# A decoder layer's start: the first adaLN columns move from VectorE to TensorE, and the small vectors ride with x

## The chip, the cores and the metric

The kernel runs on one core of a Trainium2 chip. A core has five engines with a queue each: TensorE (PE in the profile; PEld is its loading of the stationary operand), VectorE (DVE), ScalarE (ACT), GpSimd (POOL) and SyncE (SP, which here only issues transfers), and 16 DMA engines that move data between the chip's memory and the on-chip buffers. Times are device microseconds of the program, the median of several runs.

## The reference

The layer works on 256 rows of 1,024 numbers. A conditioning vector c gives, through one big matrix, nine groups of 1,024 numbers (shift, scale and gate of three sub-layers); each sub-layer normalises, scales and shifts its input, and its output is gated and added back.

```
mod = (silu(c) @ w_ada + b_ada)                      # 9 x 1024 numbers: sh1 sc1 gt1 sh2 ...
sh1, sc1, gt1, sh2, sc2, gt2, sh3, sc3, gt3 = split(mod, 9)
n = rmsnorm(h, g_ffn1) * (1 + sc1) + sh1
h = h + 0.5 * gt1 * ((silu(n @ w1_gate) * (n @ w1_up)) @ w1_down)
n = rmsnorm(h, g_mix) * (1 + sc2) + sh2
h = h + gt2 * hybrid_mixer(n)                        # pooling + dilated attention
n = rmsnorm(h, g_ffn2) * (1 + sc3) + sh3
h = h + 0.5 * gt3 * swiglu(n, w2_gate, w2_up, w2_down)
return rmsnorm(h, g_final)
```

All inputs are float32. Each large product is made of three TensorE products of rounded parts, so every weight tile is first split into `hi` (rounded, a cast) and `lo` (what the rounding lost, a subtraction), and so is every activation tile (`nh`, `nl`).

## The kernel before

**One stream of weights.** All weights lie in memory as 114 units of 128 x 2,048 numbers (1 MB each), in the order in which they are used (`plan`). `fetch` issues the transfer of one unit from SP into one of four buffers `raw` (L274). A unit of kind `ada` holds two blocks of 128 columns of `w_ada`, turned so that a column of the result lies on a partition: VectorE multiplies each block (128 x 1,024) with `cb`, the vector silu(c) repeated on all partitions, and sums along the row (L279), which gives two columns of `mod`. Any other unit is cast to `hi` by ScalarE (L290) and subtracted to `lo` by VectorE (L291), and its buffer is then free for the next transfer.

**The first feed-forward, one k-tile at a time.** The first products cannot wait for all of `mod`. So the first eight k-tiles (j = 0 to 7, 128 of the 1,024 inputs each) are done one after the other: an `ada` unit gives the shift and scale columns of tile j, `scale_cols` makes the factor `acol` (L377), `lead_mod` applies both to the transposed normalised rows and gives `nha` and `nla` (L463 to L466), and `lead_step` makes 24 products of 512 columns (L485) with the `lead` unit of the same j. Units 0 and 1 (tile 0) and 2 and 3 (tile 1) are the first four of the stream.

**The start, in a written order.** Tile 0 is written out by hand inside `in_order()` (L550 to L591), which makes each engine keep the order of the text. TensorE runs short products without use (`spin`), spreads c over the partitions (`pc`, L554), and turns the first halves of the normalised rows of both row tiles (`xt`, L318). VectorE squares and sums the rows (L561), makes `gains` (L567), the two columns of `mod` from unit 0 (L570), `acol` (L377), the first cast of unit 1 (L579), `n32` and `nla` (L582, L584), and the four `lo` pieces of unit 1 (L590). ScalarE scales the rows (L534), makes `nha` (L581), and casts the rest of unit 1 (L587) with two copies of turned rows between (L537). Behind it `casts_after` holds the casts of later units back.

**The small vectors.** The biases of `w_ada`, the three gains and `pool_scale`, 100 numbers on each partition, come as a tile of their own, `vecs`, by a transfer that ScalarE issues at the start (L204). The rows x come in two transfers from SP (L201, L203).

**Elsewhere.** The order of the rest comes from a scheduler that places instructions by priority; GpSimd issues the transfers of the mixer's tables (L775 to L777) and makes the inverse roots of the norms.

Of the kernel before, what the change touches and what calls it, by code (L numbers as in the profile page):

```python
# [15 lines left out]
P = 128  # L16
S = 256
NT = S // P
D = 1024
# [23 lines left out]
WMIX = (4, 12)  # L43
WLEAD = (0, 4)
RAW = 4
SPIN = (4, 8, 8, 5)
SPLIT = (9, 10)
GATE = 25
PARTS = 11
PAD = 336  # L50


def lead_set(f, j):
# [48 lines left out]
def pack(inp):  # L102
    def f(name):
        return np.asarray(inp[name])

    adaT = f("w_ada")[0].T.reshape(NMOD * KD, P, D)
    gu, down = [], []
    for i in (1, 2):
        g = f(f"w{i}_gate")[0].reshape(KD, P, NCH, 256)
        u = f(f"w{i}_up")[0].reshape(KD, P, NCH, 256)  # L110
        gu.append(np.stack([g, u], axis=3))
        down.append(f(f"w{i}_down")[0].reshape(NCH, 2, P, D))
    win = f("w_in")[0].reshape(2, 4, P, 4, 512)
    wout = f("w_out")[0].reshape(4, 2, P, D)
    order = plan()
    w = np.empty((len(order), P, 2048), np.float32)
    for i, (kind, a) in enumerate(order):
        if kind == "ada":
            w[i].reshape(P, 2, D)[:] = adaT[list(a)].transpose(1, 0, 2)
        elif kind == "lead":  # L120
            w[i].reshape(P, LEAD, 2, 256)[:] = gu[a[0]][a[1], :, list(lead_set(*a))].transpose(1, 0, 2, 3)
        elif kind == "gu":
            w[i].reshape(P, 4, 2, 256)[:] = gu[a[0]][4 * a[2]:4 * a[2] + 4, :, a[1]].transpose(1, 0, 2, 3)
        elif kind == "down":
            w[i].reshape(P, 2, D)[:] = down[a[0]][a[1]].transpose(1, 0, 2)
        elif kind == "win":
            w[i].reshape(P, 4, 512)[:] = win[a[1], :, :, a[0]].transpose(1, 0, 2)
        else:
            w[i].reshape(P, 2, D)[:] = wout[a].transpose(1, 0, 2)

    vec = np.concatenate([
        f("b_ada")[0].reshape(NMOD * KD, P).T,
        f("g_ffn1")[0].reshape(KD, P).T,
        f("g_mix")[0].reshape(KD, P).T,
        f("g_ffn2")[0].reshape(KD, P).T,
        f("pool_scale")[0].reshape(4, P).T,
    ], axis=1)
    x = f("x")[0].reshape(NT, P, D).transpose(1, 0, 2).reshape(P, NT * D)
    wpool = f("w_pool")[0].transpose(1, 0, 2).reshape(P, 4 * P)
    return {  # L140
        "w": w, "vec": np.ascontiguousarray(vec), "x": np.ascontiguousarray(x),
        "c": np.ascontiguousarray(f("c")), "gf": np.ascontiguousarray(f("g_final")).reshape(1, D),
        "wpool": np.ascontiguousarray(wpool), "band": band(), "bias": bias_table(),
    }
# [28 lines left out]
def block_kernel(ctx, tc, w, vec, x, c, gf, wpool, bandd, biasd, out):  # L173
# [18 lines left out]

    ffn1_pool = tc.tile_pool(name="ffn1", bufs=1, reuse_waits="tile")
    fp = [ffn1_pool.__enter__()]
    h = const.tile([P, NT * D], F32, name="h")
    cb = const.tile([P, D], F32, name="cb")
    ident = const.tile([P, P], F32, name="ident")
    lay.tile([P, PAD // 4], F32, name="lay")
    crow = work.tile([P, D], F32, name="crow", tag="gt", bufs=1)[0:1, :]
    vecs = const.tile([P, vec.shape[1]], F32, name="vecs")  # L200
    nc.sync.dma_start(h[:, 0:D], x[:, 0:D])  # L201
    nc.scalar.dma_start(crow, c)
    nc.sync.dma_start(h[:, D:2 * D], x[:, D:2 * D])  # L203
    nc.scalar.dma_start(vecs, vec)  # L204

    G1, PS = NMOD * KD, NMOD * KD + 3 * KD
    mod = const.tile([P, NMOD * KD], F32, name="mod")
    acol = const.tile([P, 3 * KD], F32, name="acol")
    make_identity(nc, ident)
    gains = const.tile([P, 3 * KD], F32, name="gains")  # L210
    mhalf = const.tile([P, 1], F32, name="mhalf")
    nc.gpsimd.memset(mhalf, -0.5)
    deps = const.tile([P, 1], F32, name="deps")
    nc.gpsimd.memset(deps, D * EPS)
    ones = work.tile([KD, P], F32, name="ones", tag="gs", bufs=1)[0:1, :]
# [53 lines left out]
    def fetch():  # L269
        i = pos[0]  # L270
        pos[0] += 1
        kind, a = order[i]
        raw = rawp.tile([P, 2048], F32, name=f"raw{i}", tag="raw")
        nc.sync.dma_start(raw, w[i])  # L274
        if kind == "ada":
            with tc.high_priority(offset=ADA if i >= 2 * KD else 0):
                for s, m in enumerate(a):
                    r = raw[:, ts(s, D)]
                    note(nc.vector.tensor_tensor_reduce(  # L279
                        r, r, cb, 1.0, vecs[:, m:m + 1], ALU.mult, ALU.add, mod[:, m:m + 1]), i, 1)  # L280
                    done_mod.add(m)
            return
        his, los = [], []
        for s in range(2):
            hi = hip.tile([P, 1024], F32R, name=f"hi{i}_{s}", tag="hi")
            lo = lop.tile([P, 1024], F32R, name=f"lo{i}_{s}", tag="lo")
            n = 1024 // (2 if i in (1, 2 * KD - 1) else 1)
            for o in range(0, 1024, n):
                src = raw[:, s * 1024 + o:s * 1024 + o + n]
                note(nc.scalar.copy(hi[:, o:o + n], src), i + s / 2, 0)  # L290
                note(nc.vector.tensor_tensor(lo[:, o:o + n], src, hi[:, o:o + n].bitcast(F32), ALU.subtract), i + s / 2, 0)  # L291
                casts[order[i], s] = bulk[-2][0].ins, bulk[-1][0].ins
            his.append(hi)
            los.append(lo)
        ready[(kind, a)] = (his, los)
# [233 lines left out]
    def spin(n):  # L529
        for _ in range(n):  # L530
            mm(spin_ps, spin_in[:, 0:P], spin_in, start=True, stop=True)

    def x_rows(t, b):
        return nc.scalar.activation(xs[t][:, ts(b, 512)], h[:, t * D + b * 512:t * D + b * 512 + 512], AF.Copy, scale=rs[t])  # L534

    def x_keep(t, b, pt):
        nc.scalar.copy(xT[b][:, :, ts(t, P)], pt)  # L537

# [11 lines left out]
    with in_order() as last:  # L550
        spin(SPIN[0])
        for b in range(2):
            pc = psp.tile([P, 512], F32, name=f"pc{b}", tag="ps")
            mm(pc, ones, crow[:, ts(b, 512)], start=True, stop=True)  # L554
            nc.scalar.activation(cb[:, ts(b, 512)], pc, AF.Silu)
        for t in range(NT):
            spin(SPIN[1 + t])
            xs.append(hip.tile([P, D], F32, name=f"xs{t}", tag="hi"))
            v = tiny.tile([P, 1], F32, name=f"vx{t}", tag="v")
            ht = h[:, ts(t, D)]  # L560
            nc.vector.tensor_tensor_reduce(xs[t], ht, ht, 1.0, D * EPS, ALU.mult, ALU.add, v)  # L561
            rs.append(tiny.tile([P, 1], F32, name=f"rx{t}", tag="r"))
            nc.gpsimd.tensor_tensor(rs[t], v, mhalf, ALU.pow)
            x_rows(t, 0)
            turned.append(turn(xs[t][:, 0:512], f"xt{t}0"))
        spin(SPIN[3])
        nc.vector.tensor_scalar(gains, vecs[:, G1:PS], float(D) ** 0.5, None, ALU.mult)  # L567
        for s, m in enumerate(order[0][1]):
            r = raw[0][:, ts(s, D)]
            nc.vector.tensor_tensor_reduce(r, r, cb, 1.0, vecs[:, m:m + 1], ALU.mult, ALU.add, mod[:, m:m + 1])  # L570
            done_mod.add(m)
        scale_cols(0, SC1, 0, 1)
        a, sh = acol[:, 0:1], mod[:, SH1 * KD:SH1 * KD + 1]
        n32 = work.tile([P, S], F32, name="n32l00", tag="t2", bufs=T2)
        for q in range(4):
            src = raw[1][:, ts(q, 512)]
            hi, lo = his[q // 2][:, ts(q % 2, 512)], los[q // 2][:, ts(q % 2, 512)]
            if q == 0:
                nc.vector.tensor_copy(hi, src)  # L579
                for t in range(NT):  # L580
                    nc.scalar.activation(n1[t][0][:, 0, :], turned[t][:, 0, :], AF.Identity, bias=sh, scale=a)  # L581
                    nc.vector.tensor_scalar(n32[:, ts(t, P)], turned[t][:, 0, :], a, sh, ALU.mult, ALU.add)  # L582
                for t in range(NT):
                    nc.vector.tensor_tensor(n1[t][1][:, 0, :], n32[:, ts(t, P)], n1[t][0][:, 0, :].bitcast(F32),  # L584
                                            ALU.subtract)
            else:
                nc.scalar.copy(hi, src)  # L587
                if q < 3:
                    x_keep(q - 1, 0, turned[q - 1])
            nc.vector.tensor_tensor(lo, src, hi.bitcast(F32), ALU.subtract)  # L590
# [105 lines left out]
    bias = [xp.tile([P, 4 * S], F32, name="bias0")]  # L696
    band_all = xp.tile([P, 4, 2 * P + 16], F32, name="band_all")
    wp_all = xp.tile([P, 4 * P], F32, name="wp_all")
    nc.gpsimd.dma_start(bias[0], biasd[:, 0:4 * S])

    def scores(hp):
# [52 lines left out]
    def pool_group(g, u, y):  # L754
# [8 lines left out]
        p2 = psp.tile([P, S], F32, name=f"pw{g}", tag="ps")  # L763
        mm(p2, wp, pl, start=True, stop=True)
        with urgent():
            sc = vecs[:, PS + g:PS + g + 1]
            for t in range(NT):
                nc.scalar.activation(y[t][0][:, g, :], p2[:, ts(t, P)], AF.Copy, scale=sc)
            for t in range(NT):
# [3 lines left out]
    after = finish1(1)  # L773
    bias.append(work.tile([P, 4 * S], F32, name="bias1", tag="gt", bufs=1))
    nc.gpsimd.dma_start(bias[1], biasd[:, 4 * S:8 * S])  # L775
    nc.gpsimd.dma_start(band_all, bandd)
    nc.gpsimd.dma_start(wp_all, wpool)  # L777
    QS = -DH ** -0.5
    y = [new_n(f"y{t}") for t in range(NT)]
    z = {}  # L780
# [167 lines left out]
```

## Time and profile before

| | |
|---|---|
| time, median of 3 runs (range) | 481.24 us (480.64 to 481.9) |
| the profiled execution: time, span | 481.04 us, 479.2 us |
| TensorE busy, share of the span | 469.0 us, 98% |
| weight loads of TensorE | 381.2 us, 80% |
| VectorE busy | 355.8 us, 74% |
| ScalarE busy | 260.9 us, 54% |
| bytes moved, mean rate | 126.05 MB, 263 GB/s |

The span is what the trace covers; the program's time has 1.84 us around it. A chain of waits goes back from the last instruction to what released each step. In a timeline each row has the start, the length, the engine, the line, the operation with what it writes and reads, how many instructions are merged in the row, and in brackets how long the engine had idled and what ended that.

### The profile page before, as it was taken

The page shows a single profiled execution, that of the slowest core. Times are in us where ns is not written, and L with a number is a line of the kernel's source. Part 1 is how long each engine was busy: PE and PEld are TensorE (multiplying, and loading weights), DVE is VectorE, ACT ScalarE, POOL GpSimd, SP SyncE. Part 2 cuts the span into 40 slices and gives each one's busy share as a digit, 9 for nine tenths or more (in the row PEclk, how much of TensorE's full clock was granted, in tenths as well). Part 3 has the DMA queues.
Part 4 walks back from the last instruction along what each step waited for, and adds up shares of the span by engine and source line. Part 5 has one row for each costly group of instructions (what it writes and reads, how often), then busy time and mean ns, then how long its engine had stood idle before and what let it go on. Part 6 is the DMA issues. An engine that isn't in the chain of part 4 may idle for free.

```text
span 479.2 us, 6028 instructions
## 1 busy us (share of the span) xinstructions
PE 469.0 (98%) x2188; PEld 381.2 (80%) x2188; DVE 355.8 (74%) x577; ACT 260.9 (54%) x447; POOL 13.4 (3%) x35
## 2 busy tenths in 40 slices
PE   8999999999999999999999999999999999999994
PEld 4678888888888888888878888888878888888883
DVE  4988899996987893789999868946666855655244
ACT  3686585454454460896877288845643543444121
POOL 1000000000000000110001000000000000000010
PEclk9999999999999999999999999999999999999998
DMA  8999995998988892579878944985457648630102
GB/s 302 412 349 345 358 347 186 351 420 356 351 316 329 302 379 122 221 279 377 334 284 334 346 177 178 376 324 176 176 180 271 260 191 327 230 122 0 44 1 88
DMA packets 19215, 126.05 MB, mean 263 GB/s; under 512 B 2329, under 2 KB 2865, under 8 KB 4850
## 3 DMA queue, kind: packets, MB, share of 16 engines
q1 hardware_dynamic: 17568, 121.12, 66.5%
q0 software_dynamic: 1184, 3.98, 2.4%
q10 hardware_dynamic: 434, 0.58, 0.3%
q8 instruction: 17, 0.28, 0.2%
q14 instruction: 12, 0.10, 0.1%
HBM read 124.61 MB, written 1.06 MB: 262 GB/s over the span
## 4 chain that ended last, share of the span: by engine, by line
PE 88%; ACT 5%; DMA 3%; issue 1%; DVE 1%; POOL 0%; POOLq 0%; DVEq 0%
PE accf L437 22%; PE gu L396 18%; PE gu L397 9%; PE le L485 9%; PE ld L485 8%; PE accm L829 5%; PE zp L396 4%; DMA raw<-in_w_dram 3%; PE zp L397 2%; PE ht L422 2%; ACT hi L290 2%; PE ld L396 2%; PE sh L396 2%; ACT nhb L367 1%; ACT n32b L368 1%
## 5 line engine op out<-in xcount | busy, mean ns | idle before, releaser
L291 DVE TENSOR_TENSOR lo<-raw,hi 128x1024 fp32r<-128x1024 f32 (+1 forms) x156 | 183.8, 1209 | 41.4 <-ACT hi L290 32.3
L290 ACT CAST hi<-raw 128x1024 fp32r<-128x1024 f32 (+1 forms) x156 | 158.2, 1045 | 74.9 <-DMA raw<-in_w_dram 32.3
L279 DVE CUSTOM_DVE_ANT_0 raw<-raw,cb,vecs 128x1024 f32<-128x1024 f32 x70 | 88.0, 1281 | 2.0 <-DMA raw<-in_w_dram 2.0
L437 PE MATMUL accf<-hi,hh 128*128 128x512 f32 x172 | 54.5, 394 | 0.2
L437 PE MATMUL accf<-hi,hl 128*128 128x512 f32 x172 | 54.2, 391 | 0.0
L437 PE MATMUL accf<-lo,hh 128*128 128x512 f32 x172 | 53.8, 389 | 0.0
L396 PE MATMUL gu<-hi,nhc 128*128 128x512 f32 x112 | 44.4, 396 | 0.0
L413 ACT ACTIVATE sg<-gu 128x256 f32<-128x256 f32 x24 | 9.2, 381 | 64.5 <-PE gu L397 64.5
L397 PE MATMUL gu<-lo,nhc 128*128 128x512 f32 x112 | 43.7, 390 | 0.0
L396 PE MATMUL gu<-hi,nlc 128*128 128x512 f32 x112 | 43.6, 390 | 0.0
L437 PEld LDWEIGHTS accf<-lo,hh 128*128 128x128 f32 x172 | 32.3, 188 | 6.8
L437 PEld LDWEIGHTS accf<-hi,hl 128*128 128x128 f32 x172 | 32.0, 188 | 7.2 <-DVE hl L311 0.7
L437 PEld LDWEIGHTS accf<-hi,hh 128*128 128x128 f32 x172 | 31.7, 188 | 7.2 <-ACT hh L310 1.1
L416 DVE TENSOR_TENSOR pr<-sg,gu 128x256 f32<-128x256 f32 x24 | 10.1, 419 | 33.1 <-ACT sg L413 33.1
L396 PE MATMUL gu<-hi,nha 128*128 128x512 f32 x80 | 31.7, 396 | 0.0
L397 PE MATMUL gu<-lo,nha 128*128 128x512 f32 x80 | 31.2, 390 | 0.0
L396 PE MATMUL gu<-hi,nla 128*128 128x512 f32 x80 | 31.1, 389 | 0.0
L311 DVE TENSOR_TENSOR hl<-ht,hh 128x256 fp32r<-128x256 f32 x44 | 16.5, 418 | 14.4 <-ACT hh L310 14.4
L310 ACT CAST hh<-ht 128x256 fp32r<-128x256 f32 x44 | 14.1, 379 | 23.0 <-PE ht L422 23.0
L396 PE MATMUL zp<-hi,nhb 128*128 128x512 f32 x64 | 26.1, 408 | 0.0
L397 PE MATMUL zp<-lo,nhb 128*128 128x512 f32 x64 | 25.0, 391 | 0.0
L396 PE MATMUL zp<-hi,nlb 128*128 128x512 f32 x64 | 25.0, 390 | 0.0
(193 smaller groups left out, 722.0 us busy)
## 6 DMA issues: line engine op xcount, KB each, us to landing
raw<-in_w_dram SPq DMA_DIRECT2D x112, 1024.0 KB, 5.7
raw<-in_w_dram SPq DMA_DIRECT2D x4, 512.0 KB, 7.8
gt<-gd POOLq DMA_DIRECT2D x3, 512.0 KB, 4.2
h<-in_x_dram SPq DMA_DIRECT2D x2, 512.0 KB, 4.7
bias<-in_bias_dram POOLq DMA_DIRECT2D x2, 512.0 KB, 3.7
band_all<-in_band_dram POOLq DMA_DIRECT2D x1, 544.0 KB, 3.6
gfb<-in_gf_dram POOLq DMA_DIRECT2D x1, 512.0 KB, 5.5
out_dram<-o SPq DMA_DIRECT2D x4, 128.0 KB, 2.5
```

The lines of the kernel that those rows point to most:

```text
L279: note(nc.vector.tensor_tensor_reduce(r, r, cb, 1.0, vecs[:, m:m + 1], ALU.mult, ALU.add, mod[:, m:m + 1]), i, 1)
L290: note(nc.scalar.copy(hi[:, o:o + n], src), i + s / 2, 0)
L291: note(nc.vector.tensor_tensor(lo[:, o:o + n], src, hi[:, o:o + n].bitcast(F32), ALU.subtract), i + s / 2, 0)
L310: nc.scalar.copy(hi_ap, src)
L311: nc.vector.tensor_tensor(lo_ap, src, hi_ap.bitcast(F32), ALU.subtract)
L396: return [mm(ps, nh[:, k, :], whi, start=first, stop=False), mm(ps, nl[:, k, :], whi, start=False, stop=False), mm(ps, nh[:, k, :], wlo, s ...
L397: mm(ps, nh[:, k, :], wlo, start=False, stop=last)]
L416: nc.vector.tensor_tensor(pr, sg, ps[:, 256:512], ALU.mult)
L422: nc.tensor.transpose(pt[:, i, :], pr[:, ts(i, P)], ident)
L437: steps.append(mm(accs[b], a[:, k, :], cols(ww, 2 * k + b), start=st, stop=sp))
L485: done.append(mm(banks[ci][t], n[t][a][:, j, :], cols(ww, lead_set(f, j).index(ci)), start=j == 0 and p == 0, stop=last and p == 2))
L829: steps.append(mm(acc2[t][b], a[:, k, :], cols(ww, 2 * kk + b), start=st, stop=sp))
```

## The change

Four pieces, all at or near the start:

1. Unit 0 is stored the other way round, so that a block of it can be TensorE's stationary operand. `first_mod(s)` makes one column of `mod` by eight products of 128 x 128 with one column of silu(c) each (`ccol`, made by ScalarE from c laid on partitions), adding up in one PSUM column; VectorE adds the bias from PSUM. The two multiply-and-sums of VectorE on unit 0 (L570) go. The other `ada` units stay as they were.
2. c on partitions joins the small vectors, and these come as 128 more columns of x's second half, in SP's transfer. ScalarE's transfer of `vecs` goes. `pool_scale` alone stays apart, as `psc`, in a new transfer that GpSimd issues behind the mixer's tables.
3. Unit 3 (the `lead` unit of tile 1) is cast and subtracted in pieces of 512 columns where it was 1,024.
4. Eight useless products fewer in the start (`SPIN`), and a smaller filler tile (`PAD`).

```diff
-SPIN = (4, 8, 8, 5)
+SPIN = (4, 8, 2, 3)
-PAD = 336
+PAD = 176
...
-        if kind == "ada":
+        if i == 0:
+            w[i].reshape(P, 2, KD, P)[:] = adaT[list(a)].reshape(2, P, KD, P).transpose(3, 0, 2, 1)
+        elif kind == "ada":
...
-        f("pool_scale")[0].reshape(4, P).T,
+        f("c").reshape(KD, P).T,
     ], axis=1)
-    x = f("x")[0].reshape(NT, P, D).transpose(1, 0, 2).reshape(P, NT * D)
+    x = np.zeros((P, NT * D + P), np.float32)
+    x[:, :NT * D] = f("x")[0].reshape(NT, P, D).transpose(1, 0, 2).reshape(P, NT * D)
+    x[:, NT * D:NT * D + vec.shape[1]] = vec
...
-    h = const.tile([P, NT * D], F32, name="h")
+    rows = const.tile([P, NT * D + P], F32, name="h")
+    h, vecs = rows[:, 0:NT * D], rows[:, NT * D:NT * D + P]
...
-    vecs = const.tile([P, vec.shape[1]], F32, name="vecs")
     nc.sync.dma_start(h[:, 0:D], x[:, 0:D])
     nc.scalar.dma_start(crow, c)
-    nc.sync.dma_start(h[:, D:2 * D], x[:, D:2 * D])
-    nc.scalar.dma_start(vecs, vec)
+    nc.sync.dma_start(rows[:, D:], x[:, D:])
...
+    ccol = const.tile([P, KD], F32, name="ccol")
...
-            n = 1024 // (2 if i in (1, 2 * KD - 1) else 1)
+            n = 1024 // (2 if i in (1, 3, 2 * KD - 1) else 1)
...
+    def first_mod(s):
+        for j in range(KD):
+            mm(first_ps[:, s:s + 1], raw[0][:, s * D + j * P:s * D + (j + 1) * P], ccol[:, j:j + 1],
+               start=j == 0, stop=j == KD - 1)
...
             x_rows(t, 0)
+            if t == 0:
+                nc.scalar.activation(ccol, vecs[:, CT:CT + KD], AF.Silu)
+                first_ps = psp.tile([P, 2], F32, name="first_ps", tag="ps")
+            else:
+                first_mod(0)
             turned.append(turn(xs[t][:, 0:512], f"xt{t}0"))
+        first_mod(1)
         spin(SPIN[3])
-        nc.vector.tensor_scalar(gains, vecs[:, G1:PS], float(D) ** 0.5, None, ALU.mult)
+        nc.vector.tensor_scalar(gains, vecs[:, G1:CT], float(D) ** 0.5, None, ALU.mult)
         for s, m in enumerate(order[0][1]):
-            r = raw[0][:, ts(s, D)]
-            nc.vector.tensor_tensor_reduce(r, r, cb, 1.0, vecs[:, m:m + 1], ALU.mult, ALU.add, mod[:, m:m + 1])
+            nc.vector.tensor_tensor(mod[:, m:m + 1], first_ps[:, s:s + 1], vecs[:, m:m + 1], ALU.add)
             done_mod.add(m)
...
+    psc = tiny.tile([P, 4], F32, name="psc", tag="psc", bufs=1)
...
-            sc = vecs[:, PS + g:PS + g + 1]
+            sc = psc[:, g:g + 1]
...
-    nc.gpsimd.dma_start(band_all, bandd)
+    bands = nc.gpsimd.dma_start(band_all, bandd)
     nc.gpsimd.dma_start(wp_all, wpool)
+    order_dep(nc.gpsimd.dma_start(psc, vec).ins, bands.ins, "not at the start")
```

**The order on TensorE at the start.** Before, from the last turn of the first row tile to the first product of tile 0, with the rows of seven useless products left out at the first mark and of four at the second (`spin` is a product without use, `xt` a turn of rows, `ld` a product of tile 0):

```order
L318 MATMUL xt_154<-ident,xs_148 128x128 x4
L531 LDWEIGHTS ident
L531 MATMUL spin<-ident 128x256
...
L318 MATMUL xt_173<-ident,xs_167 128x128 x4
L531 LDWEIGHTS ident
L531 MATMUL spin<-ident 128x256
...
L485 MATMUL ld_204<-hi_0_120,nha_126 128x512
```

In the changed kernel the same place, with the rows of two useless products left out (`first_ps` is the PSUM tile of the two new columns, `raw_113` unit 0):

```order
L322 MATMUL xt_155<-ident,xs_147 128x128 x4
L535 LDWEIGHTS ident
L535 MATMUL spin<-ident 128x256
L535 LDWEIGHTS ident
L535 MATMUL spin<-ident 128x256
L543 MATMUL first_ps<-ccol,raw_113 128x1 x8
L322 MATMUL xt_176<-ident,xs_162 128x128 x4
L543 MATMUL first_ps<-ccol,raw_113 128x1 x8
L535 LDWEIGHTS ident
L535 MATMUL spin<-ident 128x256
...
L489 MATMUL ld_213<-hi_0_119,nha_125 128x512
```

Eight of the new products stand ahead of the second turn and eight behind it, where useless products stood.

**The order on VectorE from `gains` to tile 1's factor.** Before (`raw_114` is unit 0, `raw_115` unit 1, `raw_212` unit 2):

```order
L567 TENSOR_SCALAR gains<-vecs 128x24
L570 ISA raw_114,mod<-raw_114,cb,vecs 128x1024
...
L377 SCALAR_TENSOR_TENSOR acol<-mod,gains 128x1
L579 CAST hi_0_120<-raw_115 128x512
...
L590 TENSOR_TENSOR lo_0_122<-raw_115,hi_0_120 128x512 x2
L590 TENSOR_TENSOR lo_1_123<-raw_115,hi_1_121 128x512 x2
L279 ISA raw_212,mod<-raw_212,cb,vecs 128x1024
...
L377 SCALAR_TENSOR_TENSOR acol<-mod,gains 128x1
L291 TENSOR_TENSOR lo_0_219<-raw_216,hi_0_218 128x1024
```

In the changed kernel (`raw_114` is now unit 1, `raw_221` unit 2, `raw_225` unit 3):

```order
L583 TENSOR_SCALAR gains<-h 128x24
L585 TENSOR_TENSOR mod<-first_ps,h 128x1 x2
L381 SCALAR_TENSOR_TENSOR acol<-mod,gains 128x1
L594 CAST hi_0_119<-raw_114 128x512
...
L605 TENSOR_TENSOR lo_0_121<-raw_114,hi_0_119 128x512 x2
L605 TENSOR_TENSOR lo_1_122<-raw_114,hi_1_120 128x512 x2
L283 ISA raw_221,mod<-raw_221,cb,h 128x1024
...
L381 SCALAR_TENSOR_TENSOR acol<-mod,gains 128x1
L295 TENSOR_TENSOR lo_0_228<-raw_225,hi_0_227 128x512 x2
```

The two multiply-and-sums ahead of the first `acol` have become two additions of 128 x 1; what stands behind `acol` up to tile 1's factor is the same, and unit 3's subtraction comes in pieces.

**The order on ScalarE around tile 1.** In the changed kernel (before, one cast of 128 x 1,024 stood where the first row here has two of 512):

```order
L294 CAST hi_0_227<-raw_225 128x512 x2
L467 ACTIVATE nha_125<-xT_123,mod,acol 128x128
L467 ACTIVATE nha_127<-xT_123,mod,acol 128x128
L468 ACTIVATE n32l_326<-xT_123,mod,acol 128x256
L294 CAST hi_1_233<-raw_225 128x512 x2
```

Both pieces of unit 3's first half stand ahead of tile 1's `nha`.

More of the change, by code (lines that the diff above doesn't have):

```diff
@@ L135, in pack @@
         f("g_ffn2")[0].reshape(KD, P).T,
-        f("pool_scale")[0].reshape(4, P).T,
+        f("c").reshape(KD, P).T,
     ], axis=1)
-    x = f("x")[0].reshape(NT, P, D).transpose(1, 0, 2).reshape(P, NT * D)
+    x = np.zeros((P, NT * D + P), np.float32)
+    x[:, :NT * D] = f("x")[0].reshape(NT, P, D).transpose(1, 0, 2).reshape(P, NT * D)
+    x[:, NT * D:NT * D + vec.shape[1]] = vec
     wpool = f("w_pool")[0].transpose(1, 0, 2).reshape(P, 4 * P)
     return {
-        "w": w, "vec": np.ascontiguousarray(vec), "x": np.ascontiguousarray(x),
+        "w": w, "vec": np.ascontiguousarray(f("pool_scale")[0].reshape(4, P).T), "x": x,
         "c": np.ascontiguousarray(f("c")), "gf": np.ascontiguousarray(f("g_final")).reshape(1, D),
@@ L199, in block_kernel @@
     crow = work.tile([P, D], F32, name="crow", tag="gt", bufs=1)[0:1, :]
-    vecs = const.tile([P, vec.shape[1]], F32, name="vecs")
     nc.sync.dma_start(h[:, 0:D], x[:, 0:D])
     nc.scalar.dma_start(crow, c)
-    nc.sync.dma_start(h[:, D:2 * D], x[:, D:2 * D])
-    nc.scalar.dma_start(vecs, vec)
-    G1, PS = NMOD * KD, NMOD * KD + 3 * KD
+    nc.sync.dma_start(rows[:, D:], x[:, D:])
+    G1, CT = NMOD * KD, (NMOD + 3) * KD
     mod = const.tile([P, NMOD * KD], F32, name="mod")
```

## The prediction

> **What bounds the kernel now.** I read the page's first part, then TensorE's waits over the whole program, then the chain of waits over the first 40 us, and at last the engines' timelines of that stretch. TensorE's waits (total, times, longest):
>
> ```profile
> PE 469.0 (98%) x2188; PEld 381.2 (80%) x2188; DVE 355.8 (74%) x577; ACT 260.9 (54%) x447; POOL 13.4 (3%) x35
> PE spin L531 <- POOL ident masks.py:199: 1.4, 1, 1.4
> PE ld L485 <- ACT nha L581: 0.9, 1, 0.9
> PE ld L485 <- ACT nha L463: 0.8, 1, 0.8
> ```
>
> TensorE has three waits in the whole program. The last is for tile 1's `nha` (L463); behind it the engine always has a product in flight until the tail. So the program's end is set by when tile 1's products start: what starts them later or earlier moves the end by the same amount, unless a later supply holds TensorE up. The chain of waits (start, length, what) says what set that start:
>
> ```profile
> 0.74 4.08 DMA h<-in_x_dram
> ...
> 4.84 12.32 DMA raw<-in_w_dram
> ...
> 17.18 0.60 ACT hi L290
> 17.78 0.35 issue
> 18.14 0.50 ACT nha L463
> 18.68 1.21 PE ld L485 x4
> ```
>
> Tile 1 starts at 18.68, behind the landing of unit 3 at 17.16, its cast and `nha`. Tile 0 and its columns of `mod` are not on this chain, though they are close. VectorE's and ScalarE's rows show how close:
>
> ```profile
> 8.52 1.28 DVE L570 CUSTOM_DVE_ANT_0 raw<-raw,cb,vecs 128x1024 f32<-128x1024 f32 x1 [0.75 <-DMA raw<-in_w_dram]
> 10.94 0.15 DVE L377 SCALAR_TENSOR_TENSOR acol<-mod,gains 128x1 f32<-128x1 f32 x1
> 11.01 0.42 DVE L579 CAST hi<-raw 128x512 fp32r<-128x512 f32 x1
> 11.68 0.76 DVE L582 TENSOR_SCALAR n32l<-xt,acol,mod 128x128 f32<-128x128 f32 x2 [0.25 <-ACT nha L581]
> 12.76 2.49 DVE L590 TENSOR_TENSOR lo<-raw,hi 128x512 fp32r<-128x512 f32 x4
> 15.16 1.28 DVE L279 CUSTOM_DVE_ANT_0 raw<-raw,cb,vecs 128x1024 f32<-128x1024 f32 x1
> 17.57 0.16 DVE L377 SCALAR_TENSOR_TENSOR acol<-mod,gains 128x1 f32<-128x1 f32 x1
> 6.82 0.72 ACT L534 ACTIVATE xs<-h,rx 128x512 f32<-128x512 f32 x1
> 11.19 0.81 ACT L581 ACTIVATE nha<-xt,mod,acol 128x128 fp32r<-128x128 f32 x2 [2.12 <-DVE acol L377]
> 11.89 0.62 ACT L587 CAST hi<-raw 128x512 fp32r<-128x512 f32 x1
> 17.18 1.05 ACT L290 CAST hi<-raw 128x1024 fp32r<-128x1024 f32 x1 [2.66 <-DMA raw<-in_w_dram]
> 18.14 0.87 ACT L463 ACTIVATE nha<-xT,mod,acol 128x128 fp32r<-128x128 f32 x2
> ```
>
> From tile 0's factor `acol` (10.94) to tile 1's (17.57) VectorE works through a fixed list and idles once, 0.25 us, for a `nha` that itself waits for `acol`. So the two factors are 17.57 - 10.94 = 6.63 us apart, and a later first one moves the second by as much. ScalarE's `nha` came 11.19 - 10.94 = 0.25 us behind `acol` for tile 0; for tile 1 that would be 17.82, and it ran at 18.14. **VectorE's chain has only 0.32 us of slack against the transfer.**
>
> **The change, part by part.** *The columns of tile 0 on TensorE.* Away go two multiply-and-sums, 10.94 - 8.52 = 2.42 us of VectorE. In come 16 calls of float32 products with one column. The nearest rows are the mixer's product with 16 columns (L759, four calls in the text) and the neighbours of one of them, and the two turns of the start:
>
> ```profile
> L759 PEld LDWEIGHTS po<-band_all,z x8: 192/192/192, 257.7 to 264.0; 128*128 128x128 f32 x8
> L759 PE MATMUL po<-band_all,z x8: 182/222/263, 257.8 to 264.1; 128*128 128x16 f32 x8
> 259.23 0.30 PEld L758 LDWEIGHTS po<-band_all,z 128*128 128x128 f32 x2
> 259.45 0.30 PEld L759 LDWEIGHTS po<-band_all,z 128*128 128x128 f32 x2
> 259.67 0.19 PEld L829 LDWEIGHTS accm<-hi,nhy 128*128 128x128 f32 x1
> 7.59 0.81 PEld L318 LDWEIGHTS xt<-ident,xs 128*128 128x128 f32 x4
> 8.39 1.17 PEld L531 LDWEIGHTS <-ident 128*128 128x128 bf16 x8
> 9.57 0.47 PEld L318 LDWEIGHTS xt<-ident,xs 128*128 128x128 f32 x4
> 15.89 1.97 PE L485 MATMUL ld<-lo,nha 128*128 128x512 f32 x8
> ```
>
> Four calls give eight loads and eight products: a float32 call is two passes. Two passes of 16 columns took from 259.45 to 259.67, 0.11 us each, and the ones of 128 columns beside them (259.23 to 259.45) took the same: the load of the 128 x 128 operand sets the pace, and a product with one column does not shorten it. So 16 passes a group, 16 x 0.11 = 1.76 us, and two groups 3.5 us. The bounds: next to nothing if the load were free and a pass cost its column alone (512 columns take 1.97 / 8 = 0.25 us), though no row shows a pass so cheap; and 0.20 us (the first turn, 0.81 / 4) if TensorE's clock is still low. I take 0.11, the only row of such a pass.
>
> The place in the order counts as much. TensorE gets to the first group behind the first turn (7.59 + 0.81 = 8.40) and two useless products (about 0.2 each at the slow pace), at 8.8; unit 0's first half is there (VectorE's L570 row waits for it until 8.52), and `ccol` is too: ScalarE makes it behind `xs` (6.82 + 0.72 = 7.54). Then 1.76, the second turn 0.47, and 1.76 again: 12.8. The last product takes 0.18 to end (L759's shortest), 13.0; the two additions and `acol` at the 0.07 us between L377 and L579 are done by 13.2 or so. Tile 0's `acol` starts at 13.2 where it was 10.94: **2.3 us later**, although VectorE has 2.42 us less to do. VectorE idles there; TensorE, which was idle or spinning, does the work more slowly than VectorE did.
>
> From here the fixed list carries it: tile 1's `acol` at 13.2 + 6.63 = 19.8, `nha` at 20.1 in place of 18.14. The cover of 0.32 us is used up and 1.95 us remain. Tile 0's own products are late by 2.3 as well, which does no more harm: they end at 15.89 + 1.97 + 2.3 = 20.2, and tile 1 starts at 18.68 + 1.95 = 20.6. The transfers behind follow: unit 4 waits for unit 0's buffer (now TensorE, 12.8, was VectorE), unit 5 for the `lo` pieces (15.16 + 2.3); they are late by what their users are.
>
> ```profile
> 206.31 0.68 POOL L777 DMA_DIRECT2D wp_all<-in_wpool_dram  x1
> L768 ACT ACTIVATE nhy<-pw,vecs x8: 360/368/372, 259.3 to 266.3; 128x128 fp32r<-128x128 f32 x8
> ```
>
> *The small vectors in x.* ScalarE issues one transfer less, and 28 columns of filler more (128 in place of 100) ride with x, under 0.02 MB of 5 MB ahead of unit 3. That can only shift the landing of units, and unit 3's landing no longer decides. Nothing, either way, in the forecast. `psc` is issued behind `wp_all` (206.31 + 0.68) and first read at 259.3: hidden by 50 us.
>
> *Unit 3 in pieces.* ScalarE casts both pieces ahead of `nha`, so `nha` gains nothing; two casts of 512 take at most 2 x 0.62 where one of 1,024 takes 1.05, under 0.2 us more. Here it is hidden: the casts end at about 18.4 and `nha` waits for VectorE until 20.1. Were unit 3 still the bound, it would cost that 0.1 to 0.2. VectorE's `lo` in two pieces is as long in sum.
>
> *Fewer useless products.* They filled waits; the three that are left run while VectorE adds. The clock is the question, below.
>
> Sum: 481.04 + 1.95 = 483.0 for the profiled execution; the runs' median stands 0.2 above that execution, so **483.2 us**. Of the 1.95 some tenths hang on the clock during the turns and on semaphore delays: 482.3 to 484.2 as this case's own range.
>
> **The rivals.** *The loads are cheap and unit 3 stays the bound (not slower).* If the passes cost next to nothing, `acol` would come at 13.2 - 3.5 = 9.7, and tile 1 would wait for unit 3 as before. It decides from about 0.05 us a pass downward (two groups in 1.6 us, `acol` by 11.3, the slack of 0.32). Then the small vectors' packets matter:
>
> ```profile
> 4.00:6.00 2.00, 2.00 (x3) 0.33 (x1) 1.15 (x2) 0.60 (x1) 0.00 (x0) 1.00 1.02 353
> 6.00:8.00 2.00, 2.00 (x11) 1.44 (x11) 1.41 (x5) 1.32 (x2) 0.79 (x2) 1.00 0.99 326
> 8.00:10.00 2.00, 2.00 (x15) 1.76 (x14) 1.48 (x3) 0.72 (x1) 0.31 (x1) 1.00 1.03 420
> ```
>
> The last column is GB/s: the four microseconds around the vectors' transfer ran at 340 where the next two ran at 420. At 420 throughout, 4 x 80 / 420 = 0.75 us would be won. So 481.24 + 0.1 - 0.75 to 481.24 + 0.1: 480.6 to 481.3. Against it stand L759's rows.
>
> *The clock is low (slower still).*
>
> ```profile
> 2.36 3.78 PE L554 MATMUL pc<-crow,ones 1*128 1x512 f32 x4
> ```
>
> The first turn's loads took 0.20 us each and the second's 0.12, with eight spins between, so the clock rose near 9 us; the one-row products of `pc` (2.36 to 6.14) had kept TensorE occupied and had not raised it. In the changed kernel the dense work ends at 8.8, just about there, and 16 passes that hardly use the array follow. If the clock rises only behind the first group, that group costs 16 x 0.09 more, 1.4 us: 484.6. If both run slow, 2.9 more and part of tile 0 at the slow pace: 486 to 488. [...]
>
> *The delay is made good.* In the first 40 us TensorE's loads waited three times for `nla`:
>
> ```profile
> PEld ld L485 <- DVE nla L466: 0.9, 3, 0.4
> ```
>
> If unit 3's earlier `lo` and the new order took these away, 483.2 - 0.9 = 482.3. Against it: `nla` waits for ScalarE's `n32`, which moves with `nha`.
>
> **How the numbers follow.** A measurement of this kernel can tell about 0.3%, 1.44 us, from no change. Chances: the forecast 0.53, cheap loads 0.24, low clock 0.13, made good 0.10. The forecast's lower end (up to 482.7) counts as no change, 0.10 of its chance; cheap loads give no change 0.16 and, if more of the stream is won than the rows show, faster 0.08; low clock is slower; made good is no change 0.09 and slower 0.01. That gives faster 0.08, within 0.3% 0.35, slower 0.57. The range leaves out the better half of the cheap loads and the worse half of the low clock: 480.7 to 485.8.
>
> **What would show it.** Right: the loads of `first_ps` 0.11 us apart; `acol` of tile 0 near 13.2 with VectorE idle from about 8 until then; unit 3's cast waiting for its transfer at about 17.2 but `nha` of tile 1 waiting for VectorE until about 20; TensorE without a wait behind 20.6. Wrong: `acol` before 11.3, or tile 1's `nha` still right behind unit 3's cast.

## The result and the profile after

The changed kernel takes 486.62 us (median of four runs, 485.66 to 487.38); the kernel before, beside it, 481.25 (480.64 to 481.9). The ratio is 1.011, 95% interval 1.0098 to 1.0122: **slower by 1.1%**. The prediction had slower as the likeliest sign, at 483.2 us, and its range ended at 485.8. Medians are of all runs; ratios leave out two runs over 1.5% above the fastest of their kernel, one of 1,673.41 us among the eleven of the first experiment and one of 493.38 us in the kernel with 24 useless products and 64 copies.

The four runs are two pairs, and the pairs differ in TensorE's mean clock: 485.66 and 486.03 us at 0.990 and 0.989, 487.2 and 487.38 us at 0.997 and 0.996. The trace after is of the first pair (485.66 us, span 483.7). Two more traces of the same kernel, taken later, turned out to be of the second.

The trace after, its chain of waits over the first 40 us (start, length, what):

```profile
6.16 1.82 PE spin L535 x8
7.98 0.85 PE xt L322 x4
8.83 0.43 PE spin L535 x2
9.26 1.79 PE first_ps L543 x16
11.05 0.50 PE xt L322 x4
11.54 1.99 PE first_ps L543 x16
13.55 0.23 DVE mod L585 x2
13.78 0.14 DVE acol L381
14.00 0.47 ACT nha L596
14.51 24.45 PE ld L489 x96
```

Before, this chain ran over the transfer of unit 3. Now it runs over TensorE's passes for the two columns, VectorE's additions, `acol` and `nha` of tile 0, and from 14.51 on through tile 0's and tile 1's products without a wait between them: tile 0 is on the path.

The engines' timelines of the same trace show what VectorE and ScalarE do meanwhile, and at what pace tile 0's products run:

```profile
13.55 0.23 DVE L585 TENSOR_TENSOR mod<-first_ps,h 128x1 f32<-128x1 f32 x2 [6.42 <-PE first_ps L543]
13.75 0.16 DVE L381 SCALAR_TENSOR_TENSOR acol<-mod,gains 128x1 f32<-128x1 f32 x1
14.51 2.08 PE L489 MATMUL ld<-hi,nha 128*128 128x512 f32 x4 [0.33 <-ACT nha L596]
17.20 1.16 ACT L294 CAST hi<-raw 128x512 fp32r<-128x512 f32 x2
18.52 1.05 PE L489 MATMUL ld<-hi,nla 128*128 128x512 f32 x2
20.39 0.16 DVE L381 SCALAR_TENSOR_TENSOR acol<-mod,gains 128x1 f32<-128x1 f32 x1
20.64 0.88 ACT L467 ACTIVATE nha<-xT,mod,acol 128x128 fp32r<-128x128 f32 x2 [2.28 <-DVE acol L381]
20.64 2.00 PE L489 MATMUL ld<-lo,nha 128*128 128x512 f32 x8
22.48 1.07 PE L489 MATMUL ld<-hi,nha 128*128 128x512 f32 x4
```

VectorE idles 6.42 us for the columns and makes tile 0's `acol` at 13.75 (10.94 before). Tile 1's follows at 20.39, which is 6.64 later (6.63 before), and its `nha` waits 2.28 us for it; unit 3's casts, at 17.20, wait for nothing on this path. So far this is the path that was predicted. But tile 1's products start at 22.48, not half a microsecond behind `nha`, because eight products of tile 0 still stand ahead of them. Two of tile 0's products at 18.52 take 1.05 us, as long as four of tile 1's at 22.48 (1.07). The windows view (the stretch, its length in us, then busy time of PE, PEld, DVE, ACT and POOL, the granted clock, DMA share, GB/s) says why:

```profile
9.40:12.75 3.35, 3.35 (x32) 3.35 (x32) 0.00 (x0) 0.00 (x0) 0.00 (x0) 1.00 1.04 435
12.80:19.60 6.80, 6.47 (x19) 4.77 (x20) 5.80 (x15) 4.36 (x9) 0.00 (x0) 0.50 0.94 343
19.65:24.00 4.35, 4.35 (x20) 3.57 (x20) 4.05 (x10) 3.36 (x7) 0.00 (x0) 1.00 0.92 384
```

**The granted clock fell to half from 12.8 to 19.6 us**, right across tile 0's products. In the trace's record of the clock it rose at 9.37, fell at 12.78 and rose again at 19.61. The record has no low clock ahead of the first rise, and the view shows that stretch as 1.00; there the pace of products of a known size must be read instead.

TensorE's waits over the whole program (total, times, longest):

```profile
PE spin L535 <- POOL ident masks.py:199: 1.4, 1, 1.4
PE po L774 <- ACT z L705: 1.2, 1, 1.2
PE ld L489 <- ACT nha L596: 0.3, 1, 0.3
```

The wait for `po` is new. I compared the start of each of TensorE's products with that of the same product before. Tile 1 is +3.80 us late, from 47 to 253 us it is +3.10 throughout, and behind the pooling products at about 260 us +4.5, which is the end's +4.62 (485.66 - 481.04) but for 0.1. Between +3.80 and +3.10 lie the three waits for `nla`, 0.9 us in sum, that TensorE's loads had before and no longer have: it comes later than their data.

### The profile page after: what moved, and what is told of

Same layout as the page of the kernel before. It is cut to its first block, busy times and chain, and to the rows that moved or that the text cites. A ratio compares the mean times of both kernels' runs of the same rounds, so it can differ in the third digit from the quotient of the medians.

```text
span 483.7 us, 6080 instructions
## 1 busy us (share of the span) xinstructions
PE 473.6 (98%) x2212; PEld 386.5 (80%) x2212; DVE 353.6 (73%) x577; ACT 260.8 (54%) x450; POOL 14.0 (3%) x36
## 4 chain that ended last, share of the span: by engine, by line
PE 87%; ACT 5%; DVE 3%; DMA 2%; issue 1%; POOL 1%; POOLq 0%; DVEq 0%; ACTq 0%
PE accf L441 22%; PE gu L400 18%; PE ld L489 10%; PE gu L401 9%; PE le L489 9%; PE accm L846 4%; PE zp L400 2%; ACT hi L294 2%; PE ht L426 2%; DMA raw<-in_w_dram 2%; PE sh L400 2%; PE ld L400 2%; PE zp L401 1%; ACT nhb L371 1%; ACT n32b L372 1%
## 5 line engine op out<-in xcount | busy, mean ns | idle before, releaser
L283 DVE CUSTOM_DVE_ANT_0 raw<-raw,cb,h 128x1024 f32<-128x1024 f32 x70 | 87.8, 1279 | 1.1 <-DMA raw<-in_w_dram 1.1
L314 ACT CAST hh<-ht 128x256 fp32r<-128x256 f32 x44 | 14.1, 379 | 19.6 <-PE ht L426 19.6
```

The source lines that it names most:

```text
L283: note(nc.vector.tensor_tensor_reduce(r, r, cb, 1.0, vecs[:, m:m + 1], ALU.mult, ALU.add, mod[:, m:m + 1]), i, 1)
L314: nc.scalar.copy(hi_ap, src)
```

## The experiments

Shifts are TensorE's against the trace before, at tile 1 and from 80 to 240 us (one number is the latter). A "group" is the work for one column of `mod`, and a "pass" one of its 16 float32 passes.

**The parts apart.** The first kernel is the change without the columns on TensorE.

```diff
-SPIN = (4, 8, 2, 3)
+SPIN = (4, 8, 8, 5)
...
-            nc.vector.tensor_tensor(mod[:, m:m + 1], first_ps[:, s:s + 1], vecs[:, m:m + 1], ALU.add)
+            r = raw[0][:, ts(s, D)]
+            nc.vector.tensor_tensor_reduce(r, r, cb, 1.0, vecs[:, m:m + 1], ALU.mult, ALU.add, mod[:, m:m + 1])
...
```

> The changed kernel with the first columns back on VectorE and all useless products back; the vectors in x and unit 3's pieces stay. Theory A (the columns on TensorE cost everything, and the vectors in x bring the stream forward by 0.65 us): tile 1's products start at about 18.0 instead of 18.68, 480.6 us, 0.1% faster than before. Rival B (the moved vectors, psc or the pieces cost the 1.2 us that TensorE lost at the pooling products): that wait is there too, 481.8 us or more.

Measured: 481.28 us (median of 11) against 481.1, ratio 1.0000, 0.9991 to 1.0009; tile 1 at 18.31 where it was 18.68, shift -0.33. Tile 1 gains half of what theory A gave it, and the runs show none of it; rival B's wait at the pooling products is not there. The loss does not come from these two edits.

The second is the other half: the columns on TensorE and the fewer useless products, with the small vectors and unit 3 as before.

```diff
-SPIN = (4, 8, 8, 5)
+SPIN = (4, 8, 2, 3)
...
+            if t == 0:
+                nc.scalar.activation(ccol, vecs[:, CT:CT + KD], AF.Silu)
+                first_ps = psp.tile([P, 2], F32, name="first_ps", tag="ps")
+            else:
+                first_mod(0)
...
+        first_mod(1)
...
```

> The kernel before with the first columns on TensorE and the eight useless products fewer, and nothing else of the change (c on partitions joins vecs in its own transfer). Theory A: as slow as the whole change, 485.5 to 487.5 us, with tile 0's acol near 13.7 and the products of tile 0 at the slow pace. Rival B: about 484.5 us, since the 1.2 us at the pooling products would be missing.

Measured: 487.49 us (483.91 to 487.91, four runs), ratio 1.0116, 1.0085 to 1.0146. The trace (487.91) is worse than the trace after, shift +6.7. Its two groups in the timeline:

```profile
10.06 3.41 PE L544 MATMUL first_ps<-ccol,raw 128*128 128x1 f32 x16
14.22 3.41 PE L544 MATMUL first_ps<-ccol,raw 128*128 128x1 f32 x16
17.87 0.16 DVE L382 SCALAR_TENSOR_TENSOR acol<-mod,gains 128x1 f32<-128x1 f32 x1
```

A pass takes 0.2 us here, not 0.11, in both groups: the clock was not up until 22.58. The time is the expected one, the path to it is not (`acol` at 17.87, not 13.7). So the clock hurts in two ways, by falling behind the groups (trace after) or by never rising ahead of them. Two of the four runs (483.91 and 487.75) have a mean clock of 0.988 and no trace.

**Does a product with one column keep the clock up?** Four of the kernels from here on stream 64 copies of the column in each pass; each pass still has its load of 128 x 128, which sets the pace (from 9.40 to 12.75 in the trace after, 32 loads and 32 products in 3.35 us, the loads back to back). The first:

```diff
-            mm(first_ps[:, s:s + 1], raw[0][:, s * D + j * P:s * D + (j + 1) * P], ccol[:, j:j + 1],
+            mm(first_ps[:, s * 64:s * 64 + 64], raw[0][:, s * D + j * P:s * D + (j + 1) * P], ccol[:, j:j + 1].to_broadcast([P, 64]),
...
```

> The whole change, but each of the 32 passes of the first columns streams 64 copies of its column where it streamed one; the loads stay as many. Theory A1 (the clock falls because passes of one column hardly use the array): the clock stays up, tile 0's products run 0.23 us each, tile 1 starts at about 21.2 where it was 22.5, and the time is 484.3 us with little spread. Theory A2 (the clock falls for another reason, such as idle time, or its fall costs nothing because VectorE sets tile 1 anyway): 485.7 to 487.4 us as the change.

Measured: 487.42 us (487.2 to 487.58, four runs), ratio 1.013, 1.0116 to 1.0144; shift +6.37. A miss: the clock rose only at 21.18, so there was nothing to keep up, and the passes took 0.2 us (two groups of 3.51 us). That the clock stays up once it is up could not be seen here.

The next leaves out half of the products on top:

```diff
-        for j in range(KD):
+        for j in range(KD // 2):
...
-               start=j == 0, stop=j == KD - 1)
+               start=j == 0, stop=j == KD // 2 - 1)
```

> As wide_64, with four products per column in place of eight: half of each sum for tile 0's shift and scale is left out. Theory A1 with the loads setting the pace: 16 loads of 0.11 us fewer, tile 0's acol 1.8 us earlier than in wide_64, tile 1 at about 19.4, 482.5 us. If the waits and the order around the groups cost the time and not the loads: acol moves by less than 0.5 us, 484 us.

Measured: 482.05 us (481.09 to 484.37, ten runs), ratio 1.0026, 1.0009 to 1.0043. The three longest (483.69 to 484.37) have no trace. The trace (481.09) has the clock up at 8.74 and shows the price of the place in the order by itself:

```profile
8.89 1.00 PE L543 MATMUL first_ps<-ccol,raw 128*128 128x64 f32 x8
10.18 1.00 PE L543 MATMUL first_ps<-ccol,raw 128*128 128x64 f32 x8
11.41 0.16 DVE L381 SCALAR_TENSOR_TENSOR acol<-mod,gains 128x1 f32<-128x1 f32 x1
18.30 0.88 ACT L467 ACTIVATE nha<-xT,mod,acol 128x128 fp32r<-128x128 f32 x2 [0.58 <-DVE acol L381]
18.85 1.20 PE L489 MATMUL ld<-hi,nha 128*128 128x512 f32 x4 [0.53 <-ACT nha L467]
```

With `acol` at 11.41 tile 1 waits for its `nha` and starts at 18.85, 7.44 later and 0.17 behind the kernel before. By the same 7.44 an `acol` at 11.24 goes with before's 18.68: the prediction's point from which the columns decide, `acol` by 11.3, holds against that start. Against the 18.31 of the first kernel it would be 10.87.

**A start with more dense products.** Two kernels run eight useless products, not two, ahead of the first group, the one with 64 copies, the other with the single column.

```diff
-SPIN = (4, 8, 2, 3)
+SPIN = (4, 8, 8, 3)
```

> The whole change with eight useless products ahead of the first group where it has two (as many as the kernel before had there), and the 64 copies of wide_64. Theory A (the late column costs some 3 us with the clock up, and everything above that is the clock): the clock rises in every execution before the first group and stays; passes 0.11 us apart, tile 0's acol at about 14.2, tile 1's first product at about 21.6, and all runs near 484.1 us, spread under 1 us. Rival C (the groups are slow in themselves, whatever goes before them): passes stay at 0.2 us, 487 us.

> As warm_wide with the change's own one-column passes. [...] Theory A2 (only the rise is at stake, a clock that is up stays up): as warm_wide, 484.1 us.

Measured: 485.73 us (485.42 to 486.06, four runs) with 64 copies where 484.1 was expected, ratio 1.0102, 1.0088 to 1.0116, shift +4.9; 486.15 (484.12 to 486.49, four runs) with one column, ratio 1.0102, 1.0085 to 1.0119, shift +4.8, where theory A2 had 484.1. The times are alike, the traces are not. First the wide kernel's windows, from its rise at 12.65 on, then the light one's, which rose at 10.53:

```profile
12.70:15.00 2.30, 2.30 (x23) 2.30 (x23) 0.00 (x0) 0.00 (x0) 0.00 (x0) 1.00 1.00 420
15.00:18.00 3.00, 2.33 (x14) 1.54 (x14) 1.87 (x9) 1.68 (x4) 0.00 (x0) 1.00 0.50 186
18.00:21.00 3.00, 3.00 (x14) 2.43 (x13) 3.00 (x5) 2.69 (x6) 0.00 (x0) 1.00 0.69 287
```

```profile
10.55:13.90 3.35, 3.35 (x32) 3.35 (x32) 0.00 (x0) 0.00 (x0) 0.00 (x0) 1.00 1.04 439
14.00:20.70 6.70, 6.37 (x19) 4.67 (x20) 5.64 (x15) 4.36 (x9) 0.00 (x0) 0.50 0.78 275
```

The light one's clock falls to 0.50 behind the stretch of one-column passes from 10.55 to 13.90, and the wide one's stays at 1.00 up to 21.00; the mean clocks of all four runs of each agree (0.990 to 0.994 light, 0.996 to 0.998 wide). The wide one won nothing by it in the end because its clock rose 2 us later and the first group ran partly slow: `acol` at 16.07, tile 1 at 23.51.

**The two small edits.** The small vectors in x alone (the first kernel with unit 3 cast whole again), and the fewer useless products alone in the kernel before:

```diff
-            n = 1024 // (2 if i in (1, 3, 2 * KD - 1) else 1)
+            n = 1024 // (2 if i in (1, 2 * KD - 1) else 1)
```

> The kernel before with the small vectors in x's second half and nothing else of the change: unit 3 is cast in one piece again. If the pieces cost what the two casts ahead of nha take (1.14 in place of 1.05 us): tile 1's first product 0.1 us earlier than in vectors_only, near 18.2, and 480.9 us. If the pieces help: it starts later than 18.31.

```diff
-SPIN = (4, 8, 8, 5)
+SPIN = (4, 8, 2, 3)
```

> The kernel before with SPIN as the change has it (eight useless products fewer) and nothing else; the first columns stay on VectorE. If the clock's rise hangs on how long the dense work goes on: some executions as before, 481.1 us, and some in which the clock rises only in tile 0's products, 483 to 484.5 us. If it is only the one-column passes that lose the clock: 481.1 us in all.

Measured: vectors alone 480.75 us (median of 11), ratio 0.9998, 0.9989 to 1.0007; fewer useless products 480.97 (median of 10), ratio 1.0002, 0.9993 to 1.0012. Neither can be told from no change. In the traces the vectors do something; timeline of the kernel with the vectors alone:

```profile
16.58 1.05 ACT L291 CAST hi<-raw 128x1024 fp32r<-128x1024 f32 x1 [2.52 <-DMA raw<-in_w_dram]
17.54 0.87 ACT L464 ACTIVATE nha<-xT,mod,acol 128x128 fp32r<-128x128 f32 x2
```

Unit 3's cast comes at 16.58 where it was 17.18, `nha` at 17.54 (18.14), tile 1 at 18.08 (18.68): -0.6. With unit 3 in pieces (the first kernel) tile 1 came at 18.31 and `nha` at 17.77, so the pieces cost 0.2 where the transfer decides. The cast begins at 17.14 in the trace of the kernel with fewer useless products and at 16.72 in the first kernel's, so both traces without the vectors' own transfer have it earlier. The runs' medians show 0.1 us of the 0.6, with an interval from -0.5 to +0.3.

**The column late, the clock full.** Twenty-four useless products at the very start, ahead of the spreading of c (`pc`), raise the clock before the columns; again with 64 copies and with one column.

```diff
-SPIN = (4, 8, 2, 3)
+SPIN = (24, 2, 2, 3)
```

> The whole change with 24 useless products at the very start (before c is spread) where it has 4, two where it has 8 behind that, and the 64 copies of wide_64: TensorE works densely from 1.4 us on, long before the first group. Theory A (with the clock up in time the late column costs 1.5 to 2 us, as the prediction's own sum had it): the clock rises by about 7 us in most executions, passes 0.11 us apart, tile 0's acol at about 12.9, tile 1 at about 20.4, 483.0 us. Rival C (the groups are slow whatever the clock, or the rise needs more than dense work): passes at 0.2 us, 486 to 487 us.

> As early_dense_wide with the change's own one-column passes. Theory A1 (one-column passes let the clock fall): it falls within 3.4 to 6.8 us of the first group, tile 0's products run at the slow pace in most executions, 484 to 486 us. Theory A2 (it does not fall when it has been up for long): as early_dense_wide, 483.0 us.

Measured with 64 copies: four runs, 483.8 and 484.01 us at a mean clock of 0.997 and 0.996, 489.91 and 493.38 at 0.982 and 0.984; ratio 1.0101, 1.0035 to 1.0166. The trace is of the run at 484.01, whose clock was up from 4.06 on:

```profile
8.67 0.42 PEld L322 LDWEIGHTS xt<-ident,xs 128*128 128x128 f32 x4 [1.25 <-ACT xs L538]
9.40 1.86 PEld L543 LDWEIGHTS first_ps<-ccol,raw 128*128 128x128 f32 x16
9.44 1.97 PE L543 MATMUL first_ps<-ccol,raw 128*128 128x64 f32 x16
11.69 1.90 PE L543 MATMUL first_ps<-ccol,raw 128*128 128x64 f32 x16
13.81 0.16 DVE L381 SCALAR_TENSOR_TENSOR acol<-mod,gains 128x1 f32<-128x1 f32 x1
20.70 0.88 ACT L467 ACTIVATE nha<-xT,mod,acol 128x128 fp32r<-128x128 f32 x2 [1.42 <-DVE acol L381]
21.25 1.20 PE L489 MATMUL ld<-hi,nha 128*128 128x512 f32 x4 [0.53 <-ACT nha L467]
```

This is the prediction's own case, with no clock in it, but for one thing: the 24 products put off `pc` and with it ScalarE's `xs` (7.91, and 6.69 in the trace after), the first turn waits for `xs`, and the first group's loads begin at 9.40 where the prediction had 8.8. Then passes of 0.11 us, `acol` at 13.81, tile 1 waiting for its `nha` and starting at 21.25, +2.57. The waits of TensorE's loads from 18 to 80 us:

```profile
PEld ld L489 <- ACT nha L467: 1.6, 4, 1.0
PEld ld L489 <- DVE nla L470: 1.0, 3, 0.4
```

Before, `nha` was waited for once in this stretch; three later waits bring the shift to +3.0, and the time to 484.0. I had expected 483.0.

With one column: 488.59 us (486.94 to 491.47, four runs, clock 0.983 to 0.986), ratio 1.0169, 1.0126 to 1.0213. The clock rose at 4.85, was low from 8.26 to 21.91, and every pass took 0.2 us; shift +7.0. There the fall came ahead of the columns, which begin at 10.18, in the stretch of the one-row products of `pc` and the wait behind them, so this pair does not test the columns. The two longer runs of the wide kernel have the mean clock of such a fall; that last is argued, no trace of them exists.

**The changed kernel again.** Its second pair of runs had no trace, and the 1.4 us between the pairs was as long as the new wait for `po`. Two more executions with a trace, with nothing edited:

> The changed kernel itself, unaltered, for a second trace. Its four runs fall in two kinds, 485.7 to 486.0 us at a mean clock of 0.99 and 487.2 to 487.4 at 0.997, and only the first kind has a trace. Theory (the clock alone): an execution of the second kind has its clock low from the start until about 20 us, with the passes of first_ps about 0.2 us apart, tile 0's acol near 17.5, tile 1's start near 25 and a shift of TensorE of +6.2 to +6.7 us against before from 40 us on, with no added wait at the pooling products; an execution of the first kind repeats the trace at hand (rise near 9.4, fall for 6.8 us, shift +3.1 at 250 us). Rival (a late supply): the clock behaves as in the trace at hand in both kinds, the shift at 250 us is +3.1 in both, and the 1.4 us between the kinds are added behind it, at the pooling products or at another wait for a weight unit.

> The same kernel once more, since one look may fall in either kind. Theory and rival as for the look before: 487.2 to 487.4 us goes with acol near 17.5, passes 0.2 us apart and a shift of +6.2 to +6.7 at 250 us (the clock), or with a shift of +3.1 at 250 us and the rest added later (a late supply).

Measured: 487.65 and 488.57 us (487.2 to 487.4 expected), beside 480.85 for the kernel before, mean clocks 0.996 and 0.997. The chain of waits of the first:

```profile
9.34 3.20 PE first_ps L543 x16
12.55 0.96 PE xt L322 x4
13.50 3.22 PE first_ps L543 x16
...
16.97 0.14 DVE acol L381
```

The first group starts at 9.34, where it started at 9.26 in the trace after; then each pass takes 0.2 us in place of 0.11, and `acol` comes at 16.94 (17.48 in the second trace, the expected 17.5). The clock rose at 21.09 and 22.92. Shifts from 80 us on: +6.7 both. In both traces the clock makes the difference to the trace after, and the rival (a late supply), which had +3.1 there, falls; the second pair's own runs have no trace. The wait for `po` is 1.2 us in the trace after, none in the first of the two, 0.5 in the second: it comes and goes in one and the same kernel. There ScalarE's copy `z` stands behind a cast that waits for a weight unit, 1.98 us in the trace after:

```profile
259.04 1.05 ACT L294 CAST hi<-raw 128x1024 fp32r<-128x1024 f32 x1 [1.98 <-DMA raw<-in_w_dram]
```

## Why the prediction was wrong

**The sign and the path were right.** `acol` of tile 0 late, VectorE's fixed list from one `acol` to the next (6.63 predicted, 6.64 or 6.65 in every trace with the columns on TensorE), `nha` of tile 1 waiting for VectorE while unit 3's cast no longer decides: all in the trace. Where the clock was up, tile 1 started 7.44 us behind tile 0's `acol` each time (11.41 to 18.85, 13.81 to 21.25, 16.07 to 23.51), so tile 0's `acol` sets the end as the sum had it.

**The step that failed is the clock**, "Fewer useless products": I took full clock for the groups and for tile 0, and made the low clock a rival with a chance of 0.13, although I had written that the clock rose "just about there". It decided in every trace of the changed kernel. In one pair of runs it is what the rival described, low through both groups and into tile 0: 487.2 to 488.6 measured, 486 to 488 priced, most of which the stated range left out. In the other pair it is something that neither forecast nor rival held: the clock rises at 9.37 and falls at 12.78, behind 3.41 us that were mostly one-column passes. I had them as "passes that hardly use the array" and drew from it only that they would not raise the clock.

**With it failed "which does no more harm"**: tile 0's products were to end at 20.2 and end at 22.64 (20.64 + 2.00), because most of the 16 that stand ahead of the last eight run at half the clock; they hold tile 1 to 22.48 where `nha` would have let it start at about 21.2.

**Term by term, for the trace after**, against 1.95: `nha` of tile 1 late by 2.50 (20.64 - 18.14; predicted 1.95), tile 0's slow products 1.3 more, together +3.80 at tile 1; 0.7 made good by the vanished waits for `nla`, +3.10; the wait for `po` +1.4. The third rival, "the delay is made good", thus had its mechanism and nearly its size (0.9 priced), but only because TensorE was later than forecast: with the full clock the waits for `nla` stayed at 1.0.

**The groups themselves were sized right.** In the kernel with 24 useless products the loads of each group take 1.73 us (9.40 to 11.13, 11.58 to 13.31) against 1.76. The timeline of TensorE's loads in the trace after shows why `acol` came at 13.75 there, 0.55 behind the forecast's 13.2:

```profile
8.84 2.12 PEld L543 LDWEIGHTS first_ps<-ccol,raw 128*128 128x128 f32 x16
10.80 0.51 PEld L322 LDWEIGHTS xt<-ident,xs 128*128 128x128 f32 x4
11.27 2.16 PEld L543 LDWEIGHTS first_ps<-ccol,raw 128*128 128x128 f32 x16
```

The first group begins at 8.84, as predicted (8.8). It takes 1.96 to the turn's load at 10.80, with its first half microsecond ahead of the clock's rise at 9.37; the second takes 1.90, to the next load at 13.17, with its last 0.4 behind the fall at 12.78; and the last product ends at half clock 0.35 behind that load, where 0.18 was allowed. So this 0.55 is the clock again.

**What the sum lacked besides.** In the kernel with 24 useless products the late column costs +2.57 at tile 1 and +3.0 in the end, not 1.95. Of the difference 0.6 is the first group's later start, which belongs to that experiment, and 0.4 comes from later waits for `nha` that the sum took for covered. Without the 0.6 tile 1 would be +2.0 late, which is an estimate and meets the 1.95; no trace has the changed kernel's own start at full clock.

**Edits at nothing.** Fewer useless products: nothing, measured, in the kernel before (ratio 1.0002); with six of them back, the changed kernel was still 1% slower. Unit 3 in pieces: 0.2 us where it decides, as written. The small vectors in x: not nothing but -0.6 us at tile 1, near the 0.75 that I had worked out from the rates and set aside; the runs can hardly tell it from nothing (ratio 0.9998), and with `acol` on the path it is covered. Two profile rows that answer to it, of DMA queue q10 (the queue of ScalarE's transfers), before and then after:

```profile
q10 hardware_dynamic: 434, 0.58, 0.3%
```

```profile
q10 hardware_dynamic: 290, 0.53, 0.3%
```

In the traces 144 packets and 0.05 MB less on this queue go with a unit 3 that comes 0.6 us earlier. Why so few bytes count so much was not shown.

**The cheap loads** (chance 0.24) are ruled out: no group of any trace averages less than 0.10 us a pass.

## What to carry to other kernels

Work that moves to an idle engine is priced by when its result arrives, not by how idle the engine was: here 2.42 us of VectorE became 3.8 to 6.4 us of TensorE ahead of the same `acol`. At a program's start, give TensorE's clock a line of its own in the sum, read from the traces when it rises and whether it falls again (here it rose between 4.06 and 22.92 us, and fell for 6.83 us behind one-column passes), and count tile after tile what follows at half pace (two products of 512 columns in 1.05 us here, where four took 1.07). When the runs of a kernel fall in groups, look at the mean clock first and take a trace of each group before explaining one.

## What the runs showed of the hardware

- **Behind back-to-back products with one column the clock fell.** TensorE was busy 3.35 of 3.35 us at 9.40 to 12.75 and the granted clock then fell to half for 6.83 us; likewise behind 10.55 to 13.90 in the light kernel with eight useless products. With 64 columns a pass, at the same pace of loads, it did not fall (the kernels with half the products, with eight and with 24 useless products ahead, in their traces). The two stretches of 3.41 us that ended in a fall held 2.9 us of one-column passes and 0.5 of other products; those of 64 columns that did not, counted in 3.41 us from the rise, held 1.5 to 2.6 of the passes and 0.8 to 1.1 of others, and that small difference was not varied by itself. The mean clocks of all four runs with eight useless products (0.990 to 0.994 with one column, 0.996 to 0.998 with 64) speak for the columns.
- **The granted clock changed in steps of 3.41 us in these traces, and where they lay differed from execution to execution.** In all 14 traces every stretch of the record that ends within the program is a whole multiple of 3.413 us: 3.41, 6.83 and 13.65, and 135, 136, 137 and 139 times it for the long ones. The first rises of the changed kernel's three traces lie 2.5, 0.6 and 2.4 us past a whole number of steps from the program's start.
- **The same start was followed by an early rise in one trace and a late one in another.** One text with starts equal to 0.1 us rose at 9.37 in one trace and at 21.09 in another. An estimate, counted back from each rise in these steps: one of them ran from 5.95 to 9.37 in the trace after and held all the dense work of the start (`spin` and the first turn, 6.09 to 9.05); in the other trace a boundary at 7.43 cut the same work into 1.3 and 1.7 us. That this cut kept the clock down was not shown, nor how much dense work a rise takes: by the same count 2.7 us of it stood ahead of the rise in the kernel with half the products, and 2.8 with a short wait inside were followed by none in the last trace until 22.92.
- **At half the clock the loads took twice as long too.** A float32 pass whose pace is its load took 0.11 us at full clock (9.40 to 12.75 in the trace after) and 0.20 to 0.21 at half (the light kernel with an early start, recorded at 0.50 from 8.26 to 21.91), so a group stretched from 1.8 to 3.2 us.
- **The mean clock of these runs tells how long it was lost after its first rise.** Half rate for 6.83 of some 480 us is 0.007 (0.997 to 0.990, trace after), for 13.65 us 0.014 (0.997 to 0.983, the light kernel with an early start). The 0.997 itself is the program's last microseconds (2.6 us at 0.50 in the trace before). What lies ahead of the first rise isn't in it: the runs at 0.997 are the slower pair.
